# Second half of x read already transposed from memory, and small square roots on VectorE instead of GpSimd, in a hybrid decoder layer

## The chip, the cores and the metric

The kernel runs on one core of a Trainium2 chip. A core has five engines that work side by side, each with its own in-order instruction queue: TensorE (PE, matmuls and transposes; its weight loads are listed as PEld), VectorE (DVE), ScalarE (ACT), GpSimd (POOL), and SyncE (SP), which only issues DMAs. The metric is device time in microseconds of the whole launch; lower is better.

## The reference, cut to what matters

One decoder layer on x of 2048 tokens by 1024 channels, everything in float32:

```
h  = RMSNorm(x); P = h @ W_in                 # columns a (q,k of window attention), b, c, u
o_A = window attention with sinks              # 4 heads
o_B = S5 state-space scan of u, GELU, GLU      # 512 channels
o_C = sparse attention: compressed + top-k selected + window branches, gated   # 4 heads
x = x + W_out @ concat(RMSNorm(o_A), RMSNorm(o_B), RMSNorm(o_C))
x = x + W_down @ relu(W_up @ RMSNorm(x))^2
```

An RMSNorm needs one factor 1/sqrt(mean square + eps) for each token; these factors are the "roots" of this case.

## The kernel before, in words

Every float32 product is made from three matmuls on operands split into a rounded high part and a remainder (`mm3`, L76 to L78): ACT casts the high part, DVE subtracts it from the source for the low part.

**The front** (`phase_front`) projects x. It works on 16 token tiles s of 128 tokens, eight in a first half and eight in a second. `load_h(s)` takes the raw tile x (tokens on partitions), turns it on PE in eight 128x128 transposes into two PSUM tiles `pt` (L116), casts the high part `hh` on ACT (L118) and subtracts the low part `hl` on DVE (L119). Its `scale` squares x on ACT with a running sum (L123) and calls `rsqrt_into` on POOL for the token factor `r`, which ACT applies when it evicts a product (L172 for u columns, L176 for a, b, c columns). `fetch(s)` issues the load of x on SP (L104) into a ring of three buffers. `product` runs the 24 matmuls of a tile with a chunk of weights; the rows of a, b and c go back to memory by DMAs on SP (L180).

The root is not an activation but eight small instructions (`rsqrt_steps`): a scaled copy (L44), an integer first guess (L45) and three Newton steps, each of two instructions for a single column (L48, L49) or of four for several columns (L51 to L54).

The second half's tiles are turned in the middle of a body of 24 products (v columns of the first half, v and u columns of the second): after the third product, `turn_in(s)` comes once a product for s = 8 to 15. Merged into the same body are 17 pair steps (`pair_steps`) that build tables of the state-space part: POOL multiplies `CA` (L483), DVE multiplies `t1` (named `ot` in the trace, one buffer, L484), POOL adds the two (L485), SP stores `CA` to memory (L489), PE multiplies it into `pk` (L493), DVE and ACT evict `pk` to `kst` (L496, L497), SP stores that. After the body come the other second-half products, merged with the scan (`ssm_steps`).

**The middle** runs window attention, GLU and compression, then `phase_mix`: 16 query tiles of sparse attention, merged with the output projection of earlier tiles (`finish_steps`), whose matmuls fill PE between attention steps. When the third query tile starts, `open_late` computes the row factors `ra` and `rc` of all 16 tiles at once, 16 columns wide (2 x 14 instructions and one halving, L1070 to L1072), sends `rc` through memory to change its layout (L1073, L1075), and PE and DVE turn it into `rb`. POOL scales the mixed rows with `ra` and `rb` (L1238). `Attn.normed` gives the tile's own norm factor: ACT squares the tile's output (L939), the root runs on `eng`, then `eng` scales (L941); `eng` is POOL for 15 tiles and DVE for the last. POOL also multiplies the softmax rows by their factors (L887, L1140), and PE transposes what POOL wrote (L900).

**The end** is the MLP: `phase_up` and `phase_down`.

The order in each engine's queue is set once, when the kernel is built: a planner takes the instructions in program order (the interleaving written out by `merge`), moves those with a priority offset, and orders the rest by its own estimate of when each is ready. On the chip each queue then runs strictly in that order and waits at each instruction for what it needs.

Of the kernel before, what the change touches and what calls it, by code (L numbers as in the profile page):

```python
# [7 lines left out]
F32 = mybir.dt.float32  # L8
# [48 lines left out]
def rsqrt_into(nc, pool, y, ss, scale, n, tag, eng=None):  # L57
    h = pool.tile([P, n], F32, tag=tag + "h", name=tag + "h")
    t = pool.tile([P, n], F32, tag=tag + "t", name=tag + "t")
    rsqrt_steps(eng or nc.vector, y, ss, h, t, scale)  # L60


def run(steps):
    for st in steps:
        st()
# [12 lines left out]
    nc.tensor.matmul(out, sl, mh, start=False, stop=last)  # L78


def phase_front(tc, C, x, norm1_g, w_in, u_st, pd, rh_a, prm, dkp, dca, pre, extra, done):

    nc = tc.nc
    with ExitStack() as ctx:
# [11 lines left out]
        pdv = {kind: t.rearrange("(c s) e -> s c e", s=T16) for kind, t in pd.items()}  # L96
        wv = w_in[0].rearrange("(k p) n -> p k n", p=P)
        g1 = sm.tile([P, NK], F32, tag="g1", name="g1", bufs=1)
        r_of, raw_x, hs = {}, {}, {}

        def fetch(s):
            if s < T16:
                raw_x[s] = xp.tile([P, D], F32, tag="x", name=f"x{s}", bufs=3)
                nc.sync.dma_start(raw_x[s], xv[s])  # L104

        def load_h(s):
            xt = raw_x.pop(s)
            p = hp[s % 8 == 7]
            hh = p.tile([P, NK, P], F32R, tag="hh", name=f"hh{s}")
            hl = p.tile([P, NK, P], F32R, tag="hl", name=f"hl{s}")  # L110
            hs[s] = hh, hl
            for half in range(2):
                pt = ps_t.tile([P, 4, P], F32, tag="pt", name=f"pt{s}_{half}")
                for j in range(4):
                    k = 4 * half + j
                    nc.tensor.transpose(pt[:, j], xt[:, k * P:(k + 1) * P], C["ident"])  # L116
                sl = slice(4 * half, 4 * half + 4)
                nc.scalar.copy(hh[:, sl], pt)  # L118
                nc.vector.tensor_tensor(hl[:, sl], pt, hh[:, sl], op=ALU.subtract)  # L119

            def scale():
                ss = xp.tile([P, 1], F32, tag="ss", name=f"ss{s}")
                nc.scalar.activation(xt, xt, AF.Square, accum_out=ss)  # L123
                r = r_of[s] = sm.tile([P, 1], F32, tag="r", name=f"r{s}", bufs=T16)
                rsqrt_into(nc, xp, r, ss, 1.0 / D, 1, "rq", nc.gpsimd)
            return scale

        def raw_w(ch, q, m, pool, bufs):
# [26 lines left out]
        def product(s, W, ch, k0=0, k1=NK, between=()):  # L155
            kind, c0, n = ch
            hh, hl = hs[s]
            if k0 == 0:
                open_[s, ch] = ps_m.tile([P, n], F32, tag="pm", name=f"pm{s}_{kind}{c0}")
            pm = open_[s, ch]  # L160
            between = list(between)
            for k in range(k0, k1):
                mm3(nc, pm, hh[:, k], hl[:, k], W[k][0], W[k][1], k == 0, k == NK - 1)
                if between:
                    between.pop(0)()
            if k1 < NK:
                return
            if kind == "u":
                r = T16 - 1 - s
                g0 = (c0 - 512) // 16  # L170
                dst = u_st[:, g0:g0 + 16, (r // 8) * P + (r % 8) * 16:(r // 8) * P + (r % 8) * 16 + 16]
                nc.scalar.activation(dst, pm.rearrange("p (g q) -> p g q", q=16), AF.Copy, scale=r_of[s])  # L172
            else:
                f, nh, step = HEADS[kind]
                o = sp.tile([P, n + nh], F32, tag="po", name=f"po{s}_{kind}", bufs=3)
                nc.scalar.activation(o[:, 0:n], pm, AF.Copy, scale=r_of[s])  # L176
                sq = sp.tile([P, 6, 64], F32, tag="sq", name=f"sq{s}_{kind}", bufs=1)[:, 0:nh]
                nc.scalar.activation(sq, o[:, f:f + nh * step].rearrange("p (h d) -> p h d", d=step)[:, :, 0:64], AF.Square)
                nc.vector.tensor_reduce(o[:, n:n + nh], sq, axis=AX.X, op=ALU.add)
                rows.append(lambda: nc.sync.dma_start(pdv[kind][s], o))  # L180
                store(1)

        rows = []
# [7 lines left out]
        def chunk(ch, half, W, nxt, parts=1):  # L191

            res = []
            ahead = list(nxt)
            for j in range(8):
                s = 8 * half + j
                for p in range(parts):
                    k0, k1 = NK * p // parts, NK * (p + 1) // parts
                    now = []
                    if ahead and j in (5, 6):  # L200
                        now = [ahead.pop(0) for _ in range(2 // parts)]
                    inner = [ahead.pop(0) for _ in range(min(len(ahead), HALF // parts))] if j == 7 else []
                    res.append(lambda s=s, k0=k0, k1=k1, inner=inner, now=now: (product(s, W, ch, k0, k1, inner), run(now)))
            return res
# [29 lines left out]
        run(merge(body, [lambda: next(gen, None)] * TABLE_PARTS))  # L234
        pairs = pair_steps(tc, C, S, dkp, dca, pre, ps_g)
        body = chunk(ch_v, 0, W[0, ch_v], []) + chunk(ch_v, 1, W[0, ch_v], steps[1, ch_u]) + chunk(ch_u, 1, W[1, ch_u], steps[1, ch_a])
        for s in range(8, 11):
            fetch(s)
        for s in range(8, T16):
# [2 lines left out]
                fetch(s + 3)  # L242
            body.insert(2 * (s - 8) + 3, turn_in)
        run(merge(body, pairs))
        done()
        tp = ctx.enter_context(tc.tile_pool(name="sg", bufs=2))
        c_b = chunk(ch_b, 1, W[1, ch_b], steps[1, ch_c], 2)
# [224 lines left out]
def pair_steps(tc, C, S, dkp, dca, tp, ps):  # L472

    nc = tc.nc
    M = {}
    NB = G // GB

    def outer(b):
        bc = [P, GB, 17, 16]
        CA = M[b] = tp.tile(bc, F32, tag="oCA", name=f"oCA{b}", bufs=2)  # L480
        t1 = tp.tile(bc, F32, tag="ot", name=f"ot{b}", bufs=1)
        ar, ai = (S[n][:, :, group_slice(b)].rearrange("p t g -> p g t").unsqueeze(3).broadcast_to(bc) for n in ("AR", "AI"))
        nc.gpsimd.tensor_tensor(CA, ar, S["C1"][:, group_slice(b)].unsqueeze(2).broadcast_to(bc), op=ALU.mult)  # L483
        nc.vector.tensor_tensor(t1, ai, S["C2"][:, group_slice(b)].unsqueeze(2).broadcast_to(bc), op=ALU.mult)  # L484
        nc.gpsimd.tensor_tensor(CA, CA, t1, op=ALU.add)  # L485

    def local(b):
        CA = M.pop(b)
        nc.sync.dma_start(dca[b], CA)  # L489
        pk = ps.tile([P, GB, 256], F32, tag="pb", name=f"pk{b}", bufs=2)  # L490
        for i in range(GB):
            g = b * GB + i
            nc.tensor.matmul(pk[:, i], S["Yp"][:, g:g + 8].rearrange("p a b -> p (a b)"), CA[:, i, 0:16].rearrange("p a b -> p (a b)"),  # L493
                             start=True, stop=True)
        kst = tp.tile([16, GB, 256], F32, tag="kst", name=f"kst{b}", bufs=1)
        nc.vector.tensor_tensor(kst[:, :, 0:16], pk[0:16, :, 0:16], S["dD"][:, group_slice(b)], op=ALU.add)  # L496
        nc.scalar.copy(kst[:, :, 16:256], pk[0:16, :, 16:256])  # L497
        nc.sync.dma_start(dkp[group_slice(b), :, 112:368].rearrange("g q c -> q g c"), kst)

    return [lambda b=b: (b < NB and outer(b), b and local(b - 1)) for b in range(NB + 1)]  # L500
# [346 lines left out]
class Attn:  # L847
# [86 lines left out]
    def normed(self, dst, o, name, eng=None):  # L934
        nc = self.nc
        eng = eng or nc.gpsimd
        ss, r = self.small(1, "ns"), self.small(1, "nr")
        flat = o.rearrange("p h d -> p (h d)")
        nc.scalar.activation(dst, flat, AF.Square, accum_out=ss)  # L939
        rsqrt_into(nc, self.sm, r, ss, 1.0 / 256, 1, "nq", eng)  # L940
        eng.tensor_scalar(dst, flat, r, 1.0, op0=ALU.mult, op1=ALU.mult)  # L941


# [80 lines left out]
def phase_mix(tc, C, x, gains, B, cmp, w_out, out_norm_g, g2, pd, oa_d, ob, x1, hT, xs, rr, rh, ss_a, ss_b, r_d, rest, release):  # L1024
    nc = tc.nc
    kcA, kcB, vc = cmp
    with ExitStack() as ctx:
# [27 lines left out]
        def open_late():  # L1055
# [11 lines left out]
            go = late["go"] = wp.tile([P, NK], F32, name="wo_g")  # L1067
            nc.sync.dma_start(go, out_norm_g[0].rearrange("(k p) -> p k", p=P))
            ra, rc = (fp.tile([P, NT], F32, name=n) for n in ("r_a", "r_c"))
            rsqrt_into(nc, sm, ra, ss_a, 1.0 / 256, NT, "ra", nc.gpsimd)  # L1070
            rsqrt_into(nc, sm, rc, ss_b, 0.25 / 512, NT, "ra", nc.gpsimd)
            nc.gpsimd.tensor_scalar(rc, rc, 0.5, 1.0, op0=ALU.mult, op1=ALU.mult)  # L1072
            nc.sync.dma_start(r_d.rearrange("(c s) -> c s", s=T16), rc)  # L1073
            rt = fp.tile([NT, P], F32, tag="pm", name="r_t", bufs=1)
            nc.sync.dma_start(rt, r_d.rearrange("(i p) -> i p", p=P))  # L1075
# [743 lines left out]
                w = nw  # L1819


def trunk(tc, x, norm1_g, w_in, qk_g, sinks, rel_bias, a_re, a_im, log_dt, b_re, b_im, c_re, c_im, d_skip, glu_w, glu_b,
          cmp_pos, cmp_w1, cmp_w2, out_norm_g, w_out, norm2_g, w_up, w_down,
          k_ident, k_anti, k_ramp, k_oh2, k_ohs, k_blk, k_forced, k_wmask, k_rows31, out, dbg=None):
    nc = tc.nc
    with ExitStack() as ctx:
# [9 lines left out]
        def late_loads(tp, ps):  # L1836
# [7 lines left out]
            for j in (0, 2):  # L1844
# [17 lines left out]
        u_st = up.tile([P, G, 256], F32, name="u_st")  # L1862
        c_pre = c_all.enter_context(ExitStack())
        pre = c_pre.enter_context(tc.tile_pool(name="pre", bufs=1, side="right"))
        phase_front(tc, C, x, norm1_g, w_in, u_st, pd, rh_a, (a_re, a_im, log_dt, b_re, b_im, c_re, c_im, d_skip), dkp, dca,
                    pre, late_loads, c_pre.close)
        c_b = c_all.enter_context(ExitStack())
        bp = c_b.enter_context(tc.tile_pool(name="bp", bufs=1, reuse_waits="tile"))
# [90 lines left out]
```

## Time and profile before

| quantity | value |
|---|---|
| median of 3 runs | 2546.9 us (2543.54 to 2548.43) |
| the profiled execution's own time | 2552.13 us |
| its span, first to last instruction | 2550.2 us |
| mean granted clock of TensorE | 0.984 |
| busy: PE, DVE, ACT, POOL | 96%, 68%, 52%, 47% |
| DMA traffic | 324.65 MB, mean 127 GB/s |

Timeline rows give the start in us, the length in us, the engine, the line, the operation, output <- inputs, and in brackets how long the engine sat idle before it and what ended that idle time. Rows of a stretch give start:end, its length, the busy time of each engine with its count of instructions, the granted clock of TensorE, the DMA engines' share and GB/s. Wait rows give who waited <- for whom: total us, times, the longest. A row of a line gives the shortest, median and longest duration in ns.

### The profile page before, as it was taken

What the parts mean: (1) busy time and instruction counts of PE and PEld (TensorE: products, weight loads), DVE (VectorE), ACT (ScalarE), POOL (GpSimd) and SP (SyncE); (2) the same over time, 40 slices, a digit from 0 to 9 for tenths busy, and PEclk for the clock granted to TensorE, in tenths of its full rate; (3) what the DMA queues carried; (4) which work ended last, traced back from release to release, by engine and by line L of the source; (5) the groups of instructions that cost most, each with busy time, mean ns of one, the idle gap of its engine ahead of it and who ended that gap; (6) DMA issues with size and microseconds to landing.
All of it is one profiled execution on the core that took longest, in us unless ns stands there. A gap on an engine that the chain in (4) does not pass through costs nothing.

```text
span 2550.2 us, 38303 instructions
## 1 busy us (share of the span) xinstructions
PE 2444.3 (96%) x12776; PEld 2065.4 (81%) x12776; DVE 1721.8 (68%) x3424; ACT 1324.6 (52%) x2767; POOL 1203.2 (47%) x1263
## 2 busy tenths in 40 slices
PE   8999999899989999899999999999999999999999
PEld 8989997677778878788778787788887888888887
DVE  4743884775587787677554545745457888888886
ACT  6334545675576566555455555654554444334442
POOL 3045222223445354454646666666554444545447
PEclk9999999998999999999999999999999999999999
DMA  6153425311121112131656677755547534444335
GB/s 200 61 127 96 125 87 163 97 58 49 44 92 51 57 51 68 55 98 55 198 193 189 191 198 210 227 160 155 148 121 261 164 102 126 133 132 132 120 101 197
DMA packets 397174, 324.65 MB, mean 127 GB/s; under 512 B 51974, under 2 KB 363916, under 8 KB 395152
## 3 DMA queue, kind: packets, MB, share of 16 engines
q1 hardware_dynamic: 360880, 297.03, 39.2%
q10 hardware_dynamic: 36096, 25.17, 3.1%
q8 instruction: 101, 1.65, 0.3%
q14 instruction: 97, 0.79, 0.1%
HBM read 209.66 MB, written 112.45 MB: 126 GB/s over the span
## 4 chain that ended last, share of the span: by engine, by line
PE 63%; DVE 5%; DMA 3%; POOL 3%; issue 3%; ACT 2%; SPq 0%; ACTq 0%; DVEq 0%; POOLq 0%
PE pdc L1755 7%; PE pdb L1755 7%; PE pda L1755 7%; PE pub L1566 6%; PE puc L1566 6%; PE pua L1566 6%; PE pdd L1755 3%; PE pud L1566 3%; PE poc L911 3%; PE pps L900 2%; PE pw L76 2%; PE pw L77 2%; PE pw L78 2%; PE pqs L876 1%; PE pqs L877 1%
## 5 line engine op out<-in xcount | busy, mean ns | idle before, releaser
L1420 ACT CAST v<-vr 128x512 fp32r<-128x512 f32 x224 | 139.4, 624 | 305.4 <-DMA vr<-vd 142.9
L1421 DVE TENSOR_TENSOR v<-vr,v 128x512 fp32r<-128x512 f32 x224 | 233.7, 1052 | 78.2 <-ACT v L1420 77.9
L1755 PE MATMUL pdc<-dw,v 128*128 128x512 f32 x768 | 187.4, 393 | 4.1 <-ACT dw L1420 3.2
L1755 PE MATMUL pda<-dw,v 128*128 128x512 f32 x768 | 184.5, 389 | 0.0
L1755 PE MATMUL pdb<-dw,v 128*128 128x512 f32 x768 | 184.5, 389 | 0.0
L1537 POOL TENSOR_TENSOR fs<-ur,ur 128x512 f32<-128x512 f32 x64 | 92.9, 1452 | 176.4 <-DMA ur<-in_w_up 131.2
L1755 PEld LDWEIGHTS pdc<-dw,v 128*128 128x128 f32 x768 | 145.5, 190 | 35.8 <-ACT dw L1420 3.6
L1755 PEld LDWEIGHTS pdb<-dw,v 128*128 128x128 f32 x768 | 144.2, 188 | 30.0
L1755 PEld LDWEIGHTS pda<-dw,v 128*128 128x128 f32 x768 | 144.1, 188 | 30.0
L1421 DVE TENSOR_TENSOR ul<-ur,uh 128x512 fp32r<-128x512 f32 x96 | 93.3, 972 | 109.8 <-ACT uh L1420 109.7
L1421 DVE TENSOR_TENSOR ul<-fs,uh 128x512 fp32r<-128x512 f32 x128 | 133.7, 1048 | 33.9 <-ACT uh L1420 33.9
L1420 ACT CAST uh<-fs 128x512 fp32r<-128x512 f32 x128 | 78.2, 621 | 141.7 <-PE pub L1566 56.4
L887 POOL TENSOR_SCALAR sls<-sls,dens,gt 128x128 f32<-128x128 f32 (+15 forms) x64 | 81.7, 1277 | 105.8 <-DVE dens L886 85.7
L903 ACT CAST ths<-pps 128x512 fp32r<-128x512 f32 (+1 forms) x144 | 79.8, 560 | 79.6 <-PE poc L911 58.1
L904 DVE TENSOR_TENSOR tls<-pps,ths 128x512 fp32r<-128x512 f32 (+1 forms) x144 | 93.8, 658 | 38.7 <-ACT ths L903 34.1
L76 PE MATMUL pw<-wo_h,mh 128*128 128x512 f32 x256 | 109.7, 428 | 7.6 <-ACT mh L1250 5.8
L900 PE MATMUL pps<-c_ident,sls 128*128 128x128 f32 x544 | 103.0, 281 | 9.1 <-POOL sls L887 5.4
L1582 POOL TENSOR_TENSOR ev<-e,e 128x512 f32<-128x512 f32 x64 | 98.3, 1535 | 27.9 <-ACT e L1579 16.8
L887 POOL TENSOR_SCALAR slw<-slw,denw,gt 128x640 f32<-128x640 f32 (+4 forms) x64 | 52.9, 827 | 122.1 <-DVE denw L886 98.5
L78 PE MATMUL pw<-wo_h,ml 128*128 128x512 f32 x256 | 105.0, 411 | 2.1 <-DVE ml L1251 2.1
L77 PE MATMUL pw<-wo_l,mh 128*128 128x512 f32 x256 | 106.4, 416 | 0.0
L1566 PE MATMUL puc<-fh,uh 128*128 128x512 f32 x256 | 101.0, 395 | 5.3 <-DVE eu L1575 5.3
(562 smaller groups left out, 7960.6 us busy)
## 6 DMA issues: line engine op xcount, KB each, us to landing
vr<-vd SPq DMA_DIRECT2D x224, 256.0 KB
ur<-in_w_up SPq DMA_DIRECT2D x128, 256.0 KB
vd<-ev SPq DMA_DIRECT2D x128, 256.0 KB
vd<-e ACTq DMA_DIRECT2D x64, 256.0 KB
dr<-in_w_down SPq DMA_DIRECT2D x32, 512.0 KB
x<-in_x SPq DMA_DIRECT2D x16, 512.0 KB
mx<-in_x SPq DMA_DIRECT2D x16, 512.0 KB
x<-mx ACTq DMA_DIRECT2D x16, 512.0 KB
```

The costliest lines, as they stand in the source:

```text
L76: nc.tensor.matmul(out, sh, mh, start=first, stop=False)
L77: nc.tensor.matmul(out, sh, ml, start=False, stop=False)
L78: nc.tensor.matmul(out, sl, mh, start=False, stop=last)
L887: nc.gpsimd.tensor_scalar(x, x, den[:, h:h + 1], gate, op0=ALU.mult, op1=ALU.mult)
L900: nc.tensor.transpose(pt[:, j, hh], sls[hh][:, (b0 + j) * P:(b0 + j + 1) * P], C["ident"])
L904: nc.vector.tensor_tensor(tl[:, 0:nb], pt[:, 0:nb], th[:, 0:nb], op=ALU.subtract)
L1420: nc.scalar.copy(dh, src)
L1421: nc.vector.tensor_tensor(dl, src, dh, op=ALU.subtract)
L1537: nc.gpsimd.tensor_tensor(t, x, y, op=op)
L1566: nc.tensor.matmul(bank[b], w[:, k], h[o][:, k], start=first and k == 0 and n == 0, stop=k == HALF - 1 and n == 2, skip_group_check=True)
L1582: nc.gpsimd.tensor_tensor(tile_("v" + o), x, y, op=op)
L1755: nc.tensor.matmul(bank[b, q], x[:, q, j], y[:, j], start=first and j == 0 and n == 0, stop=j == 1 and n == 2, skip_group_check=True)
```

## The change

1. A new input `x_t` holds x of tiles 8 to 15 already turned (128 channels on partitions, 8 x 128 values each, 512 KB a tile). In the second half `fetch` loads both that tile and the plain x, `load_h` casts and subtracts straight from the loaded tile, and the 64 transposes are gone. Both live in a new pool, three buffers for the turned tile and two (it was three) for the plain x, opened after the tables are built.
2. The token factor's root of tiles 8 to 15 runs on DVE, not POOL.
3. The pair steps' addition (L485) runs on DVE, not POOL.
4. The stores of c rows of the second half are issued by ACT, not SP.
5. In `normed` the root always runs on DVE; the scaling stays on `eng`.
6. In `open_late` the roots of `ra` and `rc`, and the halving, run on DVE.

```diff
 def fetch(s):
     if s < T16:
-        raw_x[s] = xp.tile([P, D], F32, tag="x", name=f"x{s}", bufs=3)
+        if s >= 8:
+            turned_x[s] = late_p[0].tile([P, NK, P], F32, tag="xt", name=f"xt{s}", bufs=3)
+            nc.sync.dma_start(turned_x[s], xt_in[s - 8])
+        raw_x[s] = (late_p[0] if s >= 8 else xp).tile([P, D], F32, tag="x", name=f"x{s}", bufs=2 if s >= 8 else 3)
         nc.sync.dma_start(raw_x[s], xv[s])
...
 for half in range(2):
-    pt = ps_t.tile([P, 4, P], F32, tag="pt", name=f"pt{s}_{half}")
-    for j in range(4):
-        k = 4 * half + j
-        nc.tensor.transpose(pt[:, j], xt[:, k * P:(k + 1) * P], C["ident"])
     sl = slice(4 * half, 4 * half + 4)
+    if s >= 8:
+        pt = turned_x[s][:, sl]
+    else:
+        pt = ps_t.tile([P, 4, P], F32, tag="pt", name=f"pt{s}_{half}")
+        for j in range(4):
+            k = 4 * half + j
+            nc.tensor.transpose(pt[:, j], xt[:, k * P:(k + 1) * P], C["ident"])
     nc.scalar.copy(hh[:, sl], pt)
     nc.vector.tensor_tensor(hl[:, sl], pt, hh[:, sl], op=ALU.subtract)
...
-    rsqrt_into(nc, xp, r, ss, 1.0 / D, 1, "rq", nc.gpsimd)
+    rsqrt_into(nc, xp, r, ss, 1.0 / D, 1, "rq", nc.vector if s >= 8 else nc.gpsimd)
...
-    rows.append(lambda: nc.sync.dma_start(pdv[kind][s], o))
+    rows.append(lambda: (nc.scalar if s >= 8 and kind == "c" else nc.sync).dma_start(pdv[kind][s], o))
...
+c_x = ctx.enter_context(ExitStack())
+late_p.append(c_x.enter_context(tc.tile_pool(name="a_x2", bufs=1)))
 for s in range(8, 11):
     fetch(s)
...
 run(merge(body, pairs))
+c_x.close()
...
 # pair_steps
-nc.gpsimd.tensor_tensor(CA, CA, t1, op=ALU.add)
+nc.vector.tensor_tensor(CA, CA, t1, op=ALU.add)
...
 # Attn.normed
-rsqrt_into(nc, self.sm, r, ss, 1.0 / 256, 1, "nq", eng)
+rsqrt_into(nc, self.sm, r, ss, 1.0 / 256, 1, "nq")
...
 # open_late
-rsqrt_into(nc, sm, ra, ss_a, 1.0 / 256, NT, "ra", nc.gpsimd)
-rsqrt_into(nc, sm, rc, ss_b, 0.25 / 512, NT, "ra", nc.gpsimd)
-nc.gpsimd.tensor_scalar(rc, rc, 0.5, 1.0, op0=ALU.mult, op1=ALU.mult)
+rsqrt_into(nc, sm, ra, ss_a, 1.0 / 256, NT, "ra")
+rsqrt_into(nc, sm, rc, ss_b, 0.25 / 512, NT, "ra")
+nc.vector.tensor_scalar(rc, rc, 0.5, None, op0=ALU.mult)
...
 # on the host
+if n == "x":
+    host["x_t"] = _np.asarray(inputs[n])[0].reshape(P, T16, NK, P).transpose(1, 3, 2, 0)[8:]
```

More of the change, by code (lines that the diff above doesn't have):

```diff
@@ L78, in mm3, with phase_front @@
     nc.tensor.matmul(out, sl, mh, start=False, stop=last)
-def phase_front(tc, C, x, norm1_g, w_in, u_st, pd, rh_a, prm, dkp, dca, pre, extra, done):
+def phase_front(tc, C, x, xt_in, norm1_g, w_in, u_st, pd, rh_a, prm, dkp, dca, pre, extra, done):
     nc = tc.nc
@@ L98, in phase_front @@
         g1 = sm.tile([P, NK], F32, tag="g1", name="g1", bufs=1)
-        r_of, raw_x, hs = {}, {}, {}
+        r_of, raw_x, turned_x, hs, late_p = {}, {}, {}, {}, []
         def fetch(s):
             if s < T16:
-                raw_x[s] = xp.tile([P, D], F32, tag="x", name=f"x{s}", bufs=3)
+                if s >= 8:
+                    turned_x[s] = late_p[0].tile([P, NK, P], F32, tag="xt", name=f"xt{s}", bufs=3)
+                    nc.sync.dma_start(turned_x[s], xt_in[s - 8])
+                raw_x[s] = (late_p[0] if s >= 8 else xp).tile([P, D], F32, tag="x", name=f"x{s}", bufs=2 if s >= 8 else 3)
                 nc.sync.dma_start(raw_x[s], xv[s])
@@ L1819, in phase_down, with trunk @@
                 w = nw
-def trunk(tc, x, norm1_g, w_in, qk_g, sinks, rel_bias, a_re, a_im, log_dt, b_re, b_im, c_re, c_im, d_skip, glu_w, glu_b,
+def trunk(tc, x, x_t, norm1_g, w_in, qk_g, sinks, rel_bias, a_re, a_im, log_dt, b_re, b_im, c_re, c_im, d_skip, glu_w, glu_b,
           cmp_pos, cmp_w1, cmp_w2, out_norm_g, w_out, norm2_g, w_up, w_down,
@@ L1864, in trunk @@
         pre = c_pre.enter_context(tc.tile_pool(name="pre", bufs=1, side="right"))
-        phase_front(tc, C, x, norm1_g, w_in, u_st, pd, rh_a, (a_re, a_im, log_dt, b_re, b_im, c_re, c_im, d_skip), dkp, dca,
+        phase_front(tc, C, x, x_t, norm1_g, w_in, u_st, pd, rh_a, (a_re, a_im, log_dt, b_re, b_im, c_re, c_im, d_skip), dkp, dca,
                     pre, late_loads, c_pre.close)
@@ L1947 @@
     arrays, args = {}, []
-    host = {n: inputs[n] for n in _INS}
+    host = {}
+    for n in _INS:
+        host[n] = inputs[n]
+        if n == "x":
+            host["x_t"] = _np.asarray(inputs[n])[0].reshape(P, T16, NK, P).transpose(1, 3, 2, 0)[8:]
     host.update(_shape_constants())
```

## The prediction

> **What bounds the kernel now.** I read the page's head, busy line and chain first, then stretches of the two stages that the change touches, then PE's timeline and waits inside them.
>
> ```profile
> span 2550.2 us, 38303 instructions
> PE 2444.3 (96%) x12776; PEld 2065.4 (81%) x12776; DVE 1721.8 (68%) x3424; ACT 1324.6 (52%) x2767; POOL 1203.2 (47%) x1263
> PE 63%; DVE 5%; DMA 3%; POOL 3%; issue 3%; ACT 2%; SPq 0%; ACTq 0%; DVEq 0%; POOLq 0%
> ...
> 163.00:207.00 44.00, 39.54 (x301) 36.92 (x300) 16.85 (x32) 23.15 (x47) 37.23 (x67) 1.00 0.37 115
> 207.00:249.35 42.35, 42.10 (x332) 41.02 (x331) 13.33 (x25) 15.35 (x33) 19.98 (x26) 1.00 0.28 87
> 249.35:305.00 55.65, 55.56 (x350) 53.77 (x349) 49.52 (x106) 31.56 (x64) 11.80 (x10) 1.00 0.44 127
> 305.00:416.50 111.50, 110.30 (x678) 106.80 (x678) 82.26 (x185) 54.20 (x119) 27.86 (x26) 1.00 0.33 95
> 687.00:731.00 44.00, 31.36 (x167) 25.92 (x166) 30.20 (x80) 27.24 (x64) 24.81 (x60) 0.84 0.44 133
> 731.00:1240.00 509.00, 479.85 (x3014) 410.40 (x3014) 375.08 (x1126) 307.56 (x725) 244.57 (x421) 0.98 0.21 66
> ```
>
> PE is the bound nearly everywhere: 96% busy and 63% of the chain. So a microsecond counts if it is PE's own work or a gap of PE. The turning stretch (163 to 207) has POOL at 37.23 of 44 and a PE gap of 4.5 us. From 207 to 416.5 PE has 1.5 us of gaps, so what is won before 207 should arrive whole at 416.5. The stretch around `open_late` (687 to 731) is the worst: 12.6 us of gaps and a granted clock of 0.84. After it PE has 29 us of gaps in 509, with DVE at 74%.
>
> **The change part by part.** First the turning stretch: PE's turns, the waits, and the prices.
>
> ```profile
> 163.12 1.04 PE L116 MATMUL pt<-c_ident,x 128*128 128x128 f32 x8
> 163.91 0.36 PE L76 MATMUL pm_u<-wh_u,hh 128*128 128x256 f32 x1
> ...
> 173.51 1.25 PE L116 MATMUL pt<-c_ident,x 128*128 128x128 f32 x8 [1.05 <-DVE hl L119]
> 174.60 1.03 PE L493 MATMUL pk<-oCA,k_Y 128*128 128x256 f32 x4
> ...
> PE pt L116 <- DVE hl L119: 4.5, 4, 2.1
> DVE ot L484 <- POOL oCA L485: 23.4, 8, 4.1
> ...
> L484 DVE TENSOR_TENSOR ot<-k_AI,k_C x16: 701/726/1675, 147.1 to 230.7; 128x544 f32<-128x544 f32 x16
> L119 DVE TENSOR_TENSOR hl<-pt,hh x32: 675/682/693, 6.9 to 206.9; 128x512 fp32r<-128x512 f32 x32
> ...
> 205.72 0.72 POOL L44 TENSOR_SCALAR rqh<-ss 128x1 f32<-128x1 f32 x1
> ...
> 208.88 0.27 POOL L49 TENSOR_SCALAR r<-rqt,r 128x1 f32<-128x1 f32 x1
> ...
> 1260.19 0.15 DVE L44 TENSOR_SCALAR nqh<-ns 128x1 f32<-128x1 f32 x1 [0.64 <-ACT mix L939]
> ...
> 1261.99 0.21 DVE L49 TENSOR_SCALAR nr<-nqt,nr 128x1 f32<-128x1 f32 x1
> ```
>
> *Turns removed.* Eight groups of eight transposes. Four hold PE for about 0.8 us (163.12 to 163.91), four for 1.09 us (173.51 to 174.60): 7.6 us, all on the path.
>
> *The gaps of PE between them.* PE waited 4.5 us for `hl`, because `pt` has two buffers. DVE was late since its queue holds `ot` ahead of `hl`, and `ot` (one buffer) waited 23.4 us for POOL's addition. POOL does a product, an addition and a root of 3.4 us (205.72 to 209.15) a step. With the turned tile from memory nothing of `pt` is left to wait for, and with the addition on DVE `ot` waits for its own engine. The 4.5 us go. Together 12.1 us.
>
> *What is late next.* DVE: 16.85 us are busy in the stretch; it gains 8 additions at `ot`'s 0.73 us (5.8) and 8 roots at the last tile's 2.0 us (1260.19 to 1262.20; 16.0), so 38.7 us, against 44 - 12.1 = 31.9 us of PE. That would hold PE if it all had to be done there. It need not: `hl` of tile 8 is needed only by the ninth product, five products after its turn, and pair work can slip behind 207, where DVE has 29 us free. I charge 2 us; the ends are 0 and 6.8 (DVE paces the whole stretch). Front: -10 us, bounds -12 and -5.
>
> *Sources in SBUF.* `hl` was read from PSUM and never took over 0.693 us; now both inputs are in SBUF.
>
> ```profile
> 178.14 1.16 POOL L483 TENSOR_TENSOR oCA<-k_AR,k_C 128x544 f32<-128x544 f32 x1
> 178.21 1.67 DVE L484 TENSOR_TENSOR ot<-k_AI,k_C 128x544 f32<-128x544 f32 x1 [4.08 <-POOL oCA L485]
> ```
>
> When POOL's product began 0.07 us ahead, `ot` took 1.67 us, not 0.73. Eight such meetings would cost DVE 7.5 us more; if DVE paced the stretch as well, the front would end at +2 instead of -5. I take it as hidden (DVE's spare time behind 207) and leave the rest to the third case below. The Trainium skill, "SBUF — State Buffer", says that DVE operations with two SBUF inputs and GpSimd operations take turns on one shared pair of ports, held for a whole instruction. The trace agrees with the 1.67 us; by that rule all 16 new SBUF subtractions are exposed to the products that stay on POOL, but only one product falls in each step.
>
> *New loads.* Eight tiles of 512 KB, 4.2 MB, behind SP's other issues, and the plain x has one buffer less, so its third load waits on SP until ACT has squared the first, with stores of `CA` and `kst` and weight loads behind it.
>
> ```profile
> 173.00:175.00 2.00, 1.49 (x10) 1.29 (x11) 1.14 (x3) 0.79 (x2) 1.49 (x6) 1.00 1.00 272
> L104 SPq DMA_DIRECT2D x<-in_x x16: 327/332/904, 1.2 to 191.3; - x16
> L1572 ACTq DMA_DIRECT2D vd<-e x64: 366/366/431, 1310.2 to 1928.3; - x64
> ```
>
> At the 272 GB/s of full DMA engines they take 15.4 us, plus the 16.3 us (0.37 of 44) already there: 31.7 of 31.9 us. Three tiles can come before 163, and the last is not needed before some 203, so I charge nothing; without that cover it is up to 5 us. Issuing costs SP 8 x 0.33 us. ACT's casts and squares stay (23.15 of 44). The c stores cost ACT 8 x 0.37 = 2.9 us between 305 and 416.5, where it is 49% busy and the row is stored one tile late: nothing, 2.9 us uncovered.
>
> *`open_late` and the first two tiles' norms.*
>
> ```profile
> 688.85 0.20 POOL L44 TENSOR_SCALAR rah<-ss_b 128x16 f32<-128x16 f32 x1 [3.63 <-ACT gb L671]
> ...
> 698.43 0.20 POOL L1072 TENSOR_SCALAR r_c<-r_c 128x16 f32<-128x16 f32 x1
> 698.62 0.77 POOL L887 TENSOR_SCALAR sls<-sls,dens,gt 128x512 f32<-128x512 f32 x1
> 699.45 0.47 PE L900 MATMUL pps<-c_ident,sls 128*128 128x128 f32 x1 [5.39 <-POOL sls L887]
> ...
> 713.77 0.51 POOL L44 TENSOR_SCALAR nqh<-ns 128x1 f32<-128x1 f32 x1
> ...
> 718.73 1.12 PE L900 MATMUL ppc<-c_ident,slc 128*128 128x128 f32 x4 [4.36 <-POOL slc L1140]
> ...
> 699.00:702.00 3.00, 2.55 (x13) 2.56 (x14) 0.52 (x5) 2.58 (x6) 1.31 (x3) 0.50 0.64 170
> 708.00:711.00 3.00, 3.00 (x11) 2.03 (x10) 2.89 (x7) 3.00 (x7) 0.87 (x1) 0.50 0.58 189
> 719.00:722.00 3.00, 3.00 (x15) 2.91 (x15) 1.11 (x4) 1.16 (x3) 0.53 (x1) 0.58 0.27 105
> ```
>
> POOL's roots stand in its queue right ahead of the softmax scaling that PE waits for: 5.39 and 4.36 us, and behind each gap the clock is near half. Over those three rows that is 3 x (0.50 + 0.50 + 0.42) = 4.3 us more. At most 14 us. But the same 29 instructions, 16 wide, and 2 roots go to DVE:
>
> ```profile
> L51 DVE TENSOR_TENSOR hnhn<-rh_a x3: 251/257/258, 317.5 to 321.8; 128x96 f32<-128x96 f32 x3
> ```
>
> Between 0.15 us for one column and 0.26 us for 96 I take 0.18, nearest to the narrow one: 5.2 us (4.4 to 7.5), and 4.0 us for the two roots. DVE's 30.2 us of 44 become 39.4, so if all of it is needed there, the stretch can shrink by 4.6 us. I take -4.6; ends 0 (DVE stalls PE as POOL did) and -14.
>
> The Trainium skill, "TensorE: Matmul & The Clock Gate" (Part 1), says that after an idle window of about 3.4 us PE's clock is halved until a busy window has passed. The 0.50 behind the 5.39 us gap agrees. By it, a remaining gap below 3.4 us saves the cold rows too; that is the second rival below.
>
> *The other 13 norms, 731 to 1240.*
>
> ```profile
> 860.00:960.00 100.00, 93.96 (x584) 79.37 (x584) 77.11 (x238) 62.48 (x154) 47.31 (x81) 0.98 0.15 49
> 1160.00:1260.00 100.00, 97.29 (x575) 81.37 (x574) 58.33 (x131) 47.64 (x93) 50.51 (x96) 1.00 0.37 115
> ...
> PE pth L1283 <- DVE mx L1263: 6.8, 5, 1.8
> PE poc L911 <- DVE tls L904: 5.4, 2, 5.2
> ```
>
> These are PE's two longest waits from 731 to 1240; none of its waits there ends on POOL, so relieving POOL buys nothing. DVE gains 13 x 2.0 = 26 us of work, and a root waiting for ACT's square has softmax and splitting work queued behind it, for which PE waits. Between the two rows PE's gaps grow by 3.3 us for 18.8 us of DVE work, 0.18 each: +4.6 us. Ends: 0 (all in DVE's 134 free us) and 26.
>
> *Sum*: -10 - 4.6 + 4.6 = -10 us on the profiled execution's 2552.1 (2550.2 span), 2542. That execution was 5.2 us above the median, so 2537.
>
> **The rivals.** *The gaps at `open_late` vanish with their cold clock*: -10 - 14 + 4.6, 2527. For it: DVE sat idle 695 to 701 because PE did. Against: DVE is full before.
>
> *The front gain is eaten* by DVE or late loads in the turning stretch, by the 38.7 and the 31.7 us above: -5 with the rest cancelling, 2542 to 2544, the edge of what a measurement tells from no change, about 0.2% or 5 us.
>
> *DVE's roots stall PE in the query tiles*: place 731 to 1240; if each root costs PE its whole 2.0 us, -14.6 + 26 = +11, 2558. It turns the sign above 1.1 us a tile. For it: PE's waits there are DVE's. Against: the planner can lay the eight instructions between others.
>
> **How the numbers follow.** Likeliest 0.42 (2531 to 2541), gaps gone 0.18, front eaten 0.22, DVE stalls 0.18. Faster by over 0.2%: 0.42 + 0.18 + 0.05 of the third = 0.65; the third's other 0.17 and 0.03 of the last are within: 0.20; slower 0.15. The range runs from front and gaps both at their best with half of the +4.6 (2546.9 - 12 - 14 + 2) to about half of the last rival: 2522 to 2553.
>
> **What would show it.** Right: no L116 after 45 us, the first product of the a columns of the second half at about 239 instead of 249.35, `ot` no longer waiting for POOL, PE's gaps at 690 to 720 cut to about half, and DVE's busy time up by 60 to 70 us. Wrong: PE waiting for `hh` or `hl` of late loads, DVE with 29 roots in one block ahead of reciprocals, or PE's waits for DVE past 731 up by over 15 us. A changed order of the planner elsewhere would also break it.

## The result, and the profile after

The changed kernel takes 2513.5 us (median of 4 runs, 2509.5 to 2515.8), the kernel before 2547.7 on the same chip: a ratio of 0.9862 [0.9839, 0.9886]. On a second chip, where it ran once more beside other kernels, the ratio was 0.9862 [0.9849, 0.9876] (2511.8 us). That is 35 us faster, where 10 were forecast and 25 was the end of the range. Differences in us below are a ratio less one, times 2546.8 us, the median of before beside the first four experiments.

The head, busy and chain lines of the profile after; its own time was 2509.46 us:

```profile
span 2507.7 us, 38158 instructions
PE 2422.5 (97%) x12712; PEld 2045.6 (82%) x12712; DVE 1758.7 (70%) x3653; ACT 1325.5 (53%) x2767; POOL 1121.6 (45%) x1034
PE 50%; DMA 3%; issue 1%; DVE 1%; POOL 1%; ACT 1%; SPq 0%; POOLq 0%; DVEq 0%; ACTq 0%
```

The span fell by 42.5 us: 20.7 us of PE's idle time (105.9 to 85.2) and 21.8 us of its busy time, of which the 64 transposes are only 7.6. The other matmuls are as many as before (12712), so the rest of the busy time is how long they took, and the clock can account for it: the profile's clock record holds 83.3 us at half speed before and 40.8 after, and half of the difference is 21 us (in part it lies in idle time). The gap between the two profiles is wider than that between the medians, because the profiled execution of before lay 5 us above its median and that of after 4 us below.

Where it came from, by the last product of the c columns (rows of PE's instructions on `pm_c`, first before, then after), and by two stretches, from the first to the last matmul of `pw` that lies beside attention and then to the end of the mix (before, then after):

```profile
L78 PE MATMUL pm_c<-wh_c,hl x128: 336/341/347, 93.5 to 416.3; 128*128 128x396 f32 x128
...
711.80:1258.20 546.40, 510.50 (x3175) 435.82 (x3176) 395.90 (x1165) 325.24 (x761) 264.80 (x449) 0.98 0.23 73
1258.20:1290.60 32.40, 22.44 (x82) 16.88 (x81) 18.06 (x25) 12.59 (x20) 17.99 (x25) 0.79 0.63 203
```

```profile
L78 PE MATMUL pm_c<-wh_c,hl x128: 336/341/347, 93.4 to 406.9; 128*128 128x396 f32 x128
...
690.00:1219.60 529.60, 505.20 (x3178) 429.39 (x3178) 409.44 (x1272) 322.77 (x759) 235.16 (x342) 1.00 0.24 75
1219.60:1246.20 26.60, 20.75 (x82) 15.68 (x81) 16.57 (x25) 12.44 (x20) 18.90 (x20) 0.87 0.68 228
```

The front ends 9.4 us earlier, close to the forecast 10. The query tiles, from 711.8 to 1290.6 before, are 22.6 us shorter, where the forecast had a loss of 4.6 us from the norms; DVE is busier there by 12 us and POOL less busy by 29. Another 12.4 us lie between the last c product and `pw`, and the MLP behind gives 1.9 back.

### The profile page after: what moved, and what is told of

Its sections match the earlier page's. It is cut to its first block, busy times and chain, and to the rows that moved or that the text cites. A ratio compares the mean times of both kernels' runs of the same rounds, so it can differ in the third digit from the quotient of the medians.

```text
span 2507.7 us, 38158 instructions
## 1 busy us (share of the span) xinstructions
PE 2422.5 (97%) x12712; PEld 2045.6 (82%) x12712; DVE 1758.7 (70%) x3653; ACT 1325.5 (53%) x2767; POOL 1121.6 (45%) x1034
## 4 chain that ended last, share of the span: by engine, by line
PE 50%; DMA 3%; issue 1%; DVE 1%; POOL 1%; ACT 1%; SPq 0%; POOLq 0%; DVEq 0%; ACTq 0%
PE pdc L1764 7%; PE pdb L1764 7%; PE pda L1764 7%; PE pub L1575 7%; PE puc L1575 6%; PE pua L1575 6%; PE pdd L1764 3%; PE pud L1575 3%; DMA fl<-sums 1%; PE poc L920 0%; PE pps L909 0%; PE pw L76 0%; PE pw L78 0%; PE pw L77 0%; DMA fl<-hT 0%
## 5 line engine op out<-in xcount | busy, mean ns | idle before, releaser
L1575 PE MATMUL pub<-fh,uh 128*128 128x512 f32 x256 | 102.4, 400 | 1.8 <-DVE e L1584 1.6
L1575 PE MATMUL pua<-fh,uh 128*128 128x512 f32 x256 | 101.6, 397 | 2.6 <-ACT e L1595 2.6
```

The lines of the kernel that those rows point to most:

```text
L1575: nc.tensor.matmul(bank[b], w[:, k], h[o][:, k], start=first and k == 0 and n == 0, stop=k == HALF - 1 and n == 2, skip_group_check=True)
```

## The experiments

**First the parts in groups.** Against the changed kernel, `e1_front` undoes parts 5 and 6, `e3_front_norm` part 6, `e4_front_open` part 5; `e2_mix` is the kernel before with parts 5 and 6.

```diff
 # e1_front, e4_front_open, on the changed kernel
-rsqrt_into(nc, self.sm, r, ss, 1.0 / 256, 1, "nq")
+rsqrt_into(nc, self.sm, r, ss, 1.0 / 256, 1, "nq", eng)
 # e1_front, e3_front_norm, on the changed kernel
-rsqrt_into(nc, sm, ra, ss_a, 1.0 / 256, NT, "ra")
+rsqrt_into(nc, sm, ra, ss_a, 1.0 / 256, NT, "ra", nc.gpsimd)
 ...
```

> Parts 1 to 4 alone (turned x, the second half's token roots and the pair addition on VectorE, c stores on ScalarE); the norm roots and the row-factor roots stay on GpSimd. The order of TensorE's queue differs from before only in the turning stretch and in the first 250 rows after the front. If the unforecast 25 us come from the norm roots (theory POOL): about -12 us, 9 of it by the end of the front, and the half-speed time of TensorE behind 460 us stays as before, some 75 us. If they come from the new order just behind the front (theory order): about -18 us. If they come from less half-speed time wherever TensorE's short gaps change (theory clock): -12 us and half of whatever half-speed time goes; the time and half the half-speed time must move together.

> Parts 5 and 6 alone (norm roots and row-factor roots on VectorE); the front is that of before. Queues are those of before up to about 600 us. Theory POOL: -15 to -25 us, all behind 690 us. Theory order: about -5 us. Theory clock: a plain gain of 5 to 8 us from the two gaps at 699 and 719, and half of the half-speed time that goes behind 690 us, which before has 41 us of: -10 to -25 us, in step with it.

> The changed kernel with the row-factor roots of open_late back on GpSimd. Theory POOL (norm roots do it): within 6 us of the changed kernel. If the row-factor roots do it: back to the front's gain alone, about -12 us against before.

> The changed kernel with the 15 norm roots back on GpSimd. Theory POOL: loses 15 to 25 us against the changed kernel. The prediction's own step (13 roots on VectorE cost 4.6 us) would make it 0 to 5 us faster than the changed kernel. Theory clock: no fixed side; the difference is half of the difference in half-speed time.

Measured: `e1_front` 0.9931 [0.9916, 0.9946], -17.6 us; `e2_mix` 0.9921 [0.9906, 0.9936], -20.1; `e3_front_norm` 0.9880 [0.9864, 0.9896], -30.6; `e4_front_open` 0.9923 [0.9907, 0.9938], -19.6. All four beside one another on one chip. Part 5, the norm roots, is worth 13 us on top of the front (`e3_front_norm` less `e1_front`); part 6 on top of the front (`e4_front_open` less `e1_front`) is worth 2, less than the intervals can tell from nothing. The front is worth more than its 9 us of earlier c products, and the norm roots have the other sign than forecast. These two surprises are what the other runs are about.

**The norm roots: a chain through DVE's queue.** In the prediction no wait of PE from 731 to 1240 ended on POOL. The timeline of before around its longest one shows what stands behind it:

```profile
1057.21 0.19 POOL L44 TENSOR_SCALAR nqh<-ns 128x1 f32<-128x1 f32 x1
...
1061.53 0.47 POOL L941 TENSOR_SCALAR mix<-oc,nr 128x256 f32<-128x256 f32 x1
1061.99 0.87 POOL L887 TENSOR_SCALAR slw<-slw,denw,gt 128x640 f32<-128x640 f32 x1
1062.82 0.93 POOL L1139 TENSOR_TENSOR pn<-slc,denc 128x448 f32<-128x448 f32 x1
1063.79 0.93 DVE L1147 TENSOR_REDUCE pm<-pn 128x112 f32<-128x448 f32 x1 [5.07 <-POOL pn L1139]
1064.63 1.28 DVE L904 TENSOR_TENSOR tls<-pps,ths 128x512 fp32r<-128x512 f32 x2
1065.37 0.79 PE L911 MATMUL poc<-tls,Vs 128*128 128x256 f32 x2 [5.21 <-DVE tls L904]
```

POOL spends 1057.21 to 1062.86 on the root, the scalings of the mixed rows and one of the softmax rows, then makes `pn`. DVE's reduction `pm`, next in DVE's queue, waits 5.07 us for `pn`. The splits `tls` stand behind `pm` and could not start, and PE waits 5.21 us for `tls`. The row of PE's wait names DVE; DVE was held by POOL. `e5_pn` cuts only that link: all roots stay on POOL, `pn` moves to DVE, and by a count in the two traces only about a dozen of PE's 9800 rows (equal neighbours taken as one) change place.

```diff
-nc.gpsimd.tensor_tensor(pn[:, :, 0:n], slc[:, :, 0:n], den.unsqueeze(2)..., op=ALU.mult)
+nc.vector.tensor_tensor(pn[:, :, 0:n], slc[:, :, 0:n], den.unsqueeze(2)..., op=ALU.mult)
```

> The kernel before with one instruction moved: the product pn (L1139, eight query tiles, 0.85 us each) runs on DVE, not POOL. All roots stay on POOL. Chain theory (in the query tiles POOL's roots stand ahead of pn, DVE's reduction pm waits in order for pn, the splits tls behind pm wait, and PE waits for tls, with half speed behind it): DVE's waits for pn, 9.0 us in the trace of before, are gone, so is PE's gap of 5.2 us near 1060 and the 6.8 us at half speed behind it; 5 to 8 us faster, 2539 to 2542. Theory that POOL's load as such is what counts: POOL gets 6.8 us of 1200 less, within 2 us of no change. DVE theory (each microsecond added to DVE costs PE 0.18, as in the prediction): 1 us slower.

> The kernel before with part 5 alone (the root of each tile's norm factor on DVE). If its worth does not depend on the other parts: 13 us faster, 2534, as the difference of two pairs of kernels gave. If it needs the earlier front or the roots of all tiles on DVE to pay, less: under 6 us. By the prediction's term, 4.6 us slower.

```diff
 # e6_norm, on the kernel before
-rsqrt_into(nc, self.sm, r, ss, 1.0 / 256, 1, "nq", eng)
+rsqrt_into(nc, self.sm, r, ss, 1.0 / 256, 1, "nq")
```

`e5_pn`: 0.9983 [0.9971, 0.9994], -4.3 us; `e6_norm`: 0.9954 [0.9939, 0.9969], -11.7. Waits of DVE for POOL, first in before, then in the kernel after; `e5_pn` has no such row any more:

```profile
DVE pm L1147 <- POOL pn L1139: 9.0, 4, 5.1
```

```profile
DVE pm L1156 <- POOL pn L1148: 0.8, 1, 0.8
```

So the link is real, worth 4 us by itself, with more work on DVE. But part 5 alone is worth 12 without any other part, so 8 had another source. Two kernels divide it by query tiles: the first two, whose norms lie in the stretch of `open_late`, and the others.

```diff
 # e13_norm_early (e14_norm_late: >= 2), on the kernel before
-rsqrt_into(nc, self.sm, r, ss, 1.0 / 256, 1, "nq", eng)
+rsqrt_into(nc, self.sm, r, ss, 1.0 / 256, 1, "nq", nc.vector if int(name[1:]) < 2 else eng)
```

> The kernel before with the norm factor's root on DVE for the first two query tiles only (those at 692 and 714 in the trace of before). If most of part 5's 12 us comes from the stretch of open_late, where POOL's roots stand right ahead of the scalings sls and slc (PE's gaps of 5.39 and 4.36 us): 5 to 8 us faster. If it comes from the chain of pn behind the later roots: under 2 us, since PE's 3.6 us from these gaps is given back to DVE in the same stretch.

> The kernel before with the norm factor's root on DVE for all query tiles but the first two. If most of part 5's 12 us comes from the first two tiles: what moving pn alone gave, 4 to 5 us faster, which with the first two adds up to 12. If the later roots hold more than pn's chain: 8 to 10 us faster. By the prediction's term: 4.6 us slower.

`e13_norm_early`: 0.9978 [0.9967, 0.9990], -5.6 us; `e14_norm_late`: 0.9941 [0.9929, 0.9954], -15.0. The later tiles carry it, more than either theory had. The two do not add up to `e6_norm`'s 11.7; that was another chip, and only the ends of the intervals meet (-14.2 from the two, -15.5 for `e6_norm`). The profiles settle part of this: from the last GLU matmul to the end of the mix they show 600 to 604 us in the seven kernels whose query tiles are those of before (before, `e1_front`, `e7_turn` to `e11_turn_ca`), 600 in `e13_norm_early`, 589 in `e14_norm_late` and 588 in `e6_norm`. There the first two norms add nothing, and the 13 others are worth 12 to 16 us. The same two stretches as above in `e14_norm_late`, and the first of them in `e5_pn`:

```profile
704.10:1240.90 536.80, 506.81 (x3175) 430.63 (x3176) 410.63 (x1269) 324.30 (x761) 238.55 (x351) 0.99 0.24 76
1240.90:1267.90 27.00, 21.66 (x82) 16.45 (x81) 15.64 (x25) 12.39 (x20) 15.95 (x20) 0.87 0.65 217
```

```profile
704.20:1243.70 539.50, 507.59 (x3175) 431.97 (x3176) 402.75 (x1173) 325.17 (x761) 258.76 (x443) 0.99 0.23 75
```

In the first stretch `e14_norm_late` loses 5.9 us of PE's gaps (35.9 to 30.0) and 3.7 of busy time, with DVE 14.7 us busier; in the second 5.4 us, with the clock at 0.87 for 0.79. The longest gap of the second, in before with the two ACT rows ahead of it, then in `e14_norm_late`:

```profile
1278.44 1.90 ACT L1420 CAST fh<-fl 128x2048 fp32r<-128x2048 f32 x1 [4.48 <-DMA fl<-sums]
1280.24 0.36 ACT L1250 CAST mh<-ptx 128x256 fp32r<-128x256 f32 x1
1280.66 0.80 PE L76 MATMUL pw<-wo_h,mh 128*128 128x512 f32 x1 [5.17 <-ACT mh L1250]
```

```profile
1258.22 0.50 PE L76 MATMUL pw<-wo_h,mh 128*128 128x512 f32 x1 [1.93 <-ACT mh L1250]
```

That row does not name POOL either. One link further, ACT's cast `mh` stood behind the cast `fh`, which waited 4.48 us for a load from memory, `fl` (3.93 us in `e14_norm_late`). What of POOL's work makes PE wait less there was not tried alone. Nor was another rival: when the roots change queues, the planner orders PE anew, by the same count some 130 rows in `e14_norm_late`, from 779 to 1182 us. So -15 is what the move brings, new order included.

**The first two tiles and `open_late`.** Rows of 50 us from the same point of the work: before, `e13_norm_early`, after.

```profile
685.00:735.00 50.00, 36.91 (x195) 30.12 (x194) 34.38 (x95) 30.06 (x73) 25.91 (x62) 0.86 0.42 128
```

```profile
683.00:733.00 50.00, 41.72 (x202) 34.05 (x203) 40.00 (x124) 32.56 (x79) 19.10 (x32) 0.76 0.35 116
```

```profile
665.00:715.00 50.00, 43.79 (x248) 36.38 (x247) 45.10 (x168) 35.68 (x90) 16.30 (x21) 0.86 0.43 133
...
674.03 0.50 PE L885 MATMUL pqw<-kAw,qA 128*128 128x512 f32 x1 [1.17 <-DVE nmc L888]
679.30 0.50 PE L885 MATMUL pqw<-kAw,qA 128*128 128x512 f32 x1 [2.19 <-DVE nmc L888]
687.46 1.11 PE L1257 MATMUL ptx<-c_ident,mix 128*128 128x128 f32 x4 [1.60 <-DVE ml L1260]
```

With the first two norms alone on DVE, PE's gaps shrink from 13.1 to 8.3 us, yet the clock falls from 0.86 to 0.76, which is 5.0 us of these 50. In the changed kernel 6.2 us of gaps are left, the three over 1 us for DVE, and DVE is 90% busy. Of the gap of 5.39 us, 1.74 is left with the first two norms moved and 2.48 with `open_late` moved alone (`e4_front_open`); that of 4.36 is gone in both. So each of the two moves takes away most of these two gaps, and the second adds little.

**The front, part by part.** `e7_turn` is part 1 alone, `e8_cst` part 4 alone, `e9_ca_rq` parts 2 and 3, `e11_turn_ca` parts 1 and 3, `e10_nocst` parts 1 to 3, each the lines of the diff above on the kernel before.

```diff
 # e7_turn, e10_nocst, e11_turn_ca: the lines of x_t, fetch and load_h
 # e8_cst
+rows.append(lambda: (nc.scalar if s >= 8 and kind == "c" else nc.sync).dma_start(pdv[kind][s], o))
 # e9_ca_rq, e10_nocst
+rsqrt_into(nc, xp, r, ss, 1.0 / D, 1, "rq", nc.vector if s >= 8 else nc.gpsimd)
 # e9_ca_rq, e10_nocst, e11_turn_ca
+nc.vector.tensor_tensor(CA, CA, t1, op=ALU.add)
```

> The kernel before with part 1 alone (turned tiles read from memory), additions, token roots and c stores as before. Turns theory: the 64 transposes (7.6 us) and the waits for pt (4.5 us) go whichever engine adds, so the last c product comes 8 to 9 us earlier, and the time falls by 8 to 9 us, 2538. Balance theory (DVE's ot still waits for POOL's addition, and hl behind it holds PE): 4 to 7 us only, and the rest belongs to parts 2 and 3.

> The kernel before with parts 2 and 3 alone: the transposes stay on PE, the pair steps' addition and the token roots of tiles 8 to 15 go to DVE; PE's order of work is the same. POOL-paces theory (with part 1 alone POOL was busy 24.9 of 27 us and PE only 19.4; POOL's product, addition and root set the pace of the turning stretch): without addition and root only the gaps go (4.5 us), since the transposes then fill PE again; 3 to 6 us faster, 2539 to 2542. DVE theory (DVE's ot, addition, hl and root are too much for it): 0 to 5 us slower.

> Parts 1 and 3: turned tiles and the addition on DVE, token roots left on POOL (3.4 us a tile). POOL then has a product of 1.16 and a root of 3.4 us a step, 4.6 us against PE's 4 us a step without transposes. If POOL's load paces: some 5 us of the gain of parts 1 to 3 is missing. If only DVE's wait for the addition (ot behind L494, hl behind ot) holds PE: all of it is there, since nothing in DVE's queue waits for the root.

> Parts 1, 2 and 3, c stores left on SP. POOL-paces theory: turned tiles (4 us slower alone) and the work taken off POOL pay together, 12 to 16 us faster, 2529 to 2533, and the c stores add their 2 to 4 us on top to reach the 18 of parts 1 to 4. Additive theory: the sum of parts 1 and of 2 with 3, at most 2 us faster, with the rest of the 18 owed to the c stores in combination.

> The kernel before with part 4 alone (c rows of the second half stored by ACT's queue). By the prediction 0. Queue theory: parts 1 to 4 gained 9 us after the last c product that the turning stretch does not explain, and the stores sat on SP ahead of the load of Ts for which PE waited 2.2 us at 417; moved to ACT, 2 to 3 us there, and 5 to 6 us more up to 690 where the order of PE's queue changes with this part (255 of 9394 rows): 5 to 9 us faster, 2538 to 2542. If those gains came from the earlier front instead: 0.

Measured: `e7_turn` 1.0015 [1.0004, 1.0025], 3.8 us slower; `e9_ca_rq` 0.9969 [0.9957, 0.9981], -7.9; `e11_turn_ca` 1.0011 [1.0001, 1.0021], 2.8 slower; `e10_nocst` 0.9956 [0.9940, 0.9971], -11.2; `e8_cst` 0.9986 [0.9974, 0.9999], -3.6. Rows from 163 to 207, one from each profile: `e7_turn`, `e9_ca_rq`, after.

```profile
163.00:207.00 44.00, 32.62 (x215) 30.23 (x213) 16.19 (x27) 20.00 (x40) 39.70 (x64) 0.92 0.49 167
```

```profile
163.00:207.00 44.00, 44.00 (x347) 42.88 (x346) 37.18 (x109) 24.90 (x50) 10.58 (x9) 1.00 0.40 132
```

```profile
163.00:207.00 44.00, 40.66 (x304) 38.75 (x303) 34.92 (x95) 24.46 (x50) 13.37 (x10) 1.00 0.62 209
```

Without transposes alone, POOL is busy 39.7 of 44 us and sets the pace: PE's gaps grow from 4.5 to 11.4 us, and the clock falls to 0.92. One step of it, and the longer of the two gaps over 0.2 us left in the kernel after (the other has 1.36 us, for ACT's eviction `kst`):

```profile
180.64 1.32 POOL L494 TENSOR_TENSOR oCA<-oCA,ot 128x544 f32<-128x544 f32 x1
182.00 0.73 DVE L493 TENSOR_TENSOR ot<-k_AI,k_C 128x544 f32<-128x544 f32 x1 [6.60 <-POOL oCA L494]
182.02 2.07 PE L502 MATMUL pk<-oCA,k_Y 128*128 128x256 f32 x4 [3.13 <-POOL oCA L494]
```

```profile
176.57 1.10 PE L502 MATMUL pk<-oCA,k_Y 128*128 128x256 f32 x4 [1.87 <-DVE r L49]
```

From 153 to 249 us `e7_turn` gains 7.6 us of turns and loses 7.9 in gaps (4.7 to 12.6) and 5 in clock (0.95 of 96 us): 5 us later at the end, as the profile has it (420.7 for 416.3 at the last c product). With addition and root off POOL (`e9_ca_rq`) PE has no gap left at all while it still turns. The root matters, not the addition alone: `e11_turn_ca`, with POOL's root in place, stays slower than before. Taking the turns out on top of that (`e10_nocst`) brings a further 3 us, with intervals that overlap; PE then waits for DVE's root (2.62 us once), and the clock is 0.96.

The c stores have their effect behind the front. In before the load of `Ts` is issued late on SP, behind stores that wait for c rows; PE waits for it:

```profile
399.78 7.70 SPq L180 DMA_DIRECT2D pc<-po_c  x2
...
413.99 0.38 SPq L719 DMA_DIRECT2D Ts<-rs  x1
...
419.25 1.10 PE L712 MATMUL bpfs<-Ts,c_anti 128*128 128x512 f32 x2 [2.18 <-DMA Ts<-rs]
```

In `e8_cst` the same load is issued 4.1 us before the last c matmul starts, not 2.3, and PE does not wait. From the last c matmul to the first GLU matmul (`gpm`) it takes 5.5 us instead of 8.6; `e10_nocst` takes 9.6, `e1_front` 5.5. So part 4, costed at nothing, is worth 3.6 us alone and 6.4 on top of parts 1 to 3 (`e1_front` less `e10_nocst`, two chips). In the profiles the stretch from the last c matmul to the last GLU matmul takes 257 to 264 us in the eight kernels with part 4 and 261 to 270 in the ten without, some 6 us apart on average. Part 4 also makes the planner put some 160 of PE's rows (counted as for `e5_pn`) from 393 to 480 us in another order; what that brings, beside the 3 us up to `gpm`, was not tried apart.

**A version past the changed kernel.** `pn` on DVE in the changed kernel, as in `e5_pn`, first alone, then beside the changed kernel (`e15_changed`).

> The changed kernel with the product pn of eight query tiles on DVE, not POOL. Chain theory: in the changed kernel DVE's reduction waits for pn only once, 0.8 us, so there is nothing left to free: within 2 us of the changed kernel, 2511 to 2516, though the same edit took 4 us off the kernel before. If the edit's worth came from something else than the roots ahead of pn (pn itself late on POOL): 4 us faster than the changed kernel, 2509.

> The changed kernel itself, beside the next one on one chip: about 34 us faster than before, 0.986.

> The changed kernel with pn on DVE, beside the changed kernel on the same chip. If nothing is left of the chain: within 2 us of it. If pn still holds something: 3 to 5 us faster than it, as the comparison over two chips had it.

`e12_pn_after`: 2508.0 us, 0.9846 [0.9829, 0.9863]. On one chip: `e15_changed` 2511.8, 0.9862 [0.9849, 0.9876]; `e16_changed_pn` 2508.5, 0.9850 [0.9830, 0.9870]. Some 4 and 3 us below the changed kernel, and both times within the intervals: it beats the kernel before, and whether it beats the changed one stays open.

## Why the prediction was wrong, step by step

*Turns, gaps and give-back: -10.* Right in its sum: 9.4 us at the last c product (8.9 in `e1_front`, 8.3 in `e15_changed`). The parts of the sum were not as told. PE's waits for `hl` went, but other gaps came, behind DVE's root and ACT's eviction: PE's idle time from 163 to 207 is 4.5 before and 3.3 after, where 2 were charged. And parts 2 and 3 bring 7.9 us with the turns still there (`e9_ca_rq`), the turns some 3 on top, not 7.6. The turns had been filling time that POOL's steps left free, so alone they are worth less than nothing. The reading "`ot` waits for POOL's addition" was right, but the root of 3.4 us weighed more than the addition.

*Sources in SBUF: hidden.* Right. `hl` now reads two SBUF inputs:

```profile
L125 DVE TENSOR_TENSOR hl<-pt,hh x16: 675/687/692, 7.0 to 44.8; 128x512 fp32r<-128x512 f32 x16
L125 DVE TENSOR_TENSOR hl<-xt,hh x16: 679/683/1384, 157.8 to 187.4; 128x512 fp32r<-128x512 f32 x16
```

The longest took 1.384 us, the median is 0.683 as before, and PE did not wait for any.

*Late loads: 0.* Right: DMA engines 0.62 busy from 163 to 207, and no wait of PE for `hh` or `hl`.

*c stores: 0.* Wrong, 4 to 6 us too little. The step looked at ACT, which gets the issues, and not at SP, which loses them: what stood behind them there was never priced.

*`open_late` with the first two norms: -4.6.* About right: 5.1 by `e2_mix` less `e14_norm_late`, kernels of two chips that differ in just this, with intervals of over 3 us to either side each (6.0 in the stretch from the last GLU matmul to the end of the mix of their profiles). The 16-wide instructions cost what was taken for them (0.18; the second number is the mean in ns):

```profile
L52 DVE TENSOR_TENSOR rat<-rat,rah 128x16 f32<-128x16 f32 x6 | 0.7, 158 | 0.0
L53 DVE TENSOR_SCALAR rat<-rat 128x16 f32<-128x16 f32 x6 | 0.9, 190 | 0.0
```

The clock in that stretch did not recover (0.86 both), as the likeliest case had it. The Trainium skill, "TensorE: Matmul & The Clock Gate" (Part 1), ties half speed to an idle window of about 3.4 us; by it no gap of the changed kernel there is long enough, yet the row shows 0.86.

*The other 13 norms: +4.6.* This is the step that failed. It measured -15.0 [-18.1, -11.7] (`e14_norm_late`), 20 us from the forecast, most of the 25 missed. Its premise was the wait rows: none of PE's waits ends on POOL, so relieving POOL buys nothing. A wait row names only the last link. One link further, DVE stood still in order behind `pm`, and `pm` waited for POOL 9.0 us; the prediction left that row out, as it took DVE for the bound. Moving `pn` alone brought 4.3 of the 15 us. For the rest the runs show the gain and where it lies, not its cause: less time at half speed (below), a shorter wait for `mh`, and a new order of PE's rows came together. The second premise, 0.18 us of PE for each of DVE's, came from two rows that differ in more than DVE's load: in `e14_norm_late` DVE had 14.7 us more to do and PE's gaps fell.

*DVE's load* was taken too high: 60 to 70 us more were forecast, 36.9 came. The eight instructions of a root last 1.7 us on DVE (three of 0.268 and three of 0.208, 0.148 and 0.144), not the 2.0 from its first start to its last end. For 23 roots that is some 6 us of the shortfall; the rest is not explained here. The rows of the two dearer instructions, from after:

```profile
L48 DVE TENSOR_SCALAR nqt<-nr,nqh 128x1 f32<-128x1 f32 x42 | 11.2, 268 | 0.4
L49 DVE TENSOR_SCALAR nr<-nqt,nr 128x1 f32<-128x1 f32 x42 | 8.7, 208 | 0.5
```

*What was in no step* for the query tiles is the clock. From 711.8 to 1290.6 the clock record of before has 34 us at half speed, that of `e14_norm_late` 13.7 from 704.1 to 1267.9: of the 15 us, some 10 go with it, in part as shorter busy time and in part counted as shorter gaps. It is no chance of one profile: the six kernels beside before with its query tiles have 31 to 34 us at half speed there, those with the 13 norms on DVE 11 to 21; but `e5_pn` and `e4_front_open`, with these norms on POOL, have 20 to 21 too.

The sum by these measurements: front -8 to -9, c stores -4 to -6, `open_late` with two norms -5, 13 norms -15, together -32 to -35; measured -35. It is put together from kernels of several chips, and the norms did not add up within part 5, so the single terms are good to some 4 us.

## What to carry to other kernels

A wait row names the engine that came last; before an engine is called free to load or useless to relieve, follow the wait one queue further, to what its releaser was standing behind. An instruction that moves off a queue can help everything behind it there, so a moved DMA is priced on the queue that it leaves. Work that fills another engine's pauses is not won by removing it: find what paces the stretch first, and move that.

## What the runs showed of the hardware

Half speed came without long gaps. Rows of before, and the gaps of PE of over 0.25 us in the six microseconds ahead of them: one of 1.53 us (ending at 817.11), one of 1.84 us (877.39) and, ahead of the last two rows, one of 0.57 us (599.77):

```profile
817.11 0.45 PE L900 MATMUL ppw<-c_ident,slw 128*128 128x128 f32 x1 [1.53 <-DVE tlw L904]
...
818.00:821.00 3.00, 3.00 (x14) 2.71 (x14) 2.68 (x9) 1.03 (x3) 2.60 (x7) 0.59 0.04 14
...
880.00:883.00 3.00, 3.00 (x19) 2.91 (x18) 1.28 (x5) 2.87 (x10) 0.87 (x1) 0.68 0.29 87
...
603.00:610.00 7.00, 7.00 (x28) 5.83 (x27) 4.61 (x18) 4.06 (x15) 2.96 (x6) 0.50 0.14 38
610.00:617.00 7.00, 6.68 (x26) 5.66 (x25) 3.35 (x19) 3.59 (x16) 2.60 (x5) 0.59 0.14 38
```

In the kernel after, the gap of 1.87 us at 176.57 was followed by full speed. The half-speed pieces of the clock record are multiples of 3.41 us, but for the one that the end of the kernel cuts off. Much of the scatter between executions of one kernel goes with this clock. Four experiments are the kernel before up to 690 us. In their profiles the last GLU matmul came 1.0 (`e6_norm`), 7.0 (`e14_norm_late`), 6.8 (`e5_pn`) and 10.9 us (`e13_norm_early`) earlier than in the profile of before, and from 410 us to that matmul they had 23.9, 17.1, 13.7 and 6.8 us at half speed, for 27.3 in that of before. Half of each difference in clock is 2 to 10 us. So of the 12.4 us between the last c product and `pw`, what part 4 does not explain is no more than such scatter can give. What sets the rule for short gaps, these runs don't tell.
